# Gates projected beside the attention heads, branch projections after them: one core, one encoder block in float32

## The chip, the cores and the metric

The kernel runs on one core of one Trainium2 chip. The metric is the device time in microseconds; the time of the kernel before is the median of three runs. A profile of one further execution gives the span from the first to the last instruction and, for each engine, what it did when: TensorE (PE, with its weight loads as PEld), VectorE (DVE), ScalarE (ACT), GpSimd (POOL) and SyncE (SP, which here only issues DMAs).

## The reference

One residual layer over 512 tokens of width 1024, with 16 learned meta tokens in front (528 rows, `L`). Cut to what matters here:

```python
xn = rmsnorm(h, norm_mix_g[l])
proj = xn @ w_in[l]                      # stick-breaking q, k, v and differential q, k, v, 8 heads each
...                                      # o_sb: stick-breaking attention; o_df: differential attention, normalised per head
y_sb = o_sb @ w_br_sb[l]                 # "branch projections"
y_df = o_df @ w_br_df[l]
gates = jax.nn.sigmoid(xn @ w_gate[l] + b_gate[l]).reshape(B, L_pad, 2, D)
merged = gates[:, :, 0] * y_sb + gates[:, :, 1] * y_df
h = h + merged @ w_out[l]
hn = rmsnorm(h, norm_ffn_g[l])
h = h + (jax.nn.silu(hn @ w_ffn_gate[l]) * (hn @ w_ffn_up[l])) @ w_ffn_down[l]
```

A gate for output channels f depends on `xn` alone; a branch projection for the same channels needs all eight heads of its branch.

## The kernel before, in words

Activations stand transposed: 128 channels on the partitions, tokens along the free dimension. Every float32 operand of a large product is split in two float32r parts, high (`_h`) and low (`_l`), and `mm3` (lines 284 to 289) computes a product with three matmuls: high x high (L287), high x low (L288), low x high (L289). A weight block of 128x1024 comes from DRAM through SP into one of three staging buffers (`wst`), and is split by ACT (L78, the high part `wh`) and DVE (L79, the low part `wl`) into one of four buffers. `stream` lists all weight blocks in the order of use; `stage` issues loads ahead, `prepare` splits ahead, and `weights(key)` asks for a block, which also drives both. `cols` puts a block of 128 output columns and all 8 input blocks into the stream, `rows` one of 512 output columns and 2 input blocks.

The stages follow each other. First the input is normalised and transposed into `xT_h`, `xT_l`. Then come the 8 stick-breaking heads and the 8 differential heads. While head h runs (its generator yields between its own PE steps), the loop at L1006 interleaves "units": pieces of PE work that prepare head h+1 (q, k, v projections from xT) and more pieces that are independent of the head. `n` in the loop is the number of units between two steps. A full unit for 512 tokens is 12 matmuls of 512 columns. An output larger than a unit is cut in two (`halves`: input blocks 0 to 3, then 4 to 7, into the same PSUM tile).

The further pieces are, before the change:

- at the first two heads, gates 0 of both branches (`gate_out`), kept in DRAM (`g_part`);
- from the third head on, one branch block per head: `y_units(name, i, o)` takes the results of one pair of heads (`o_h`, `o_l`, two heads in one tile), multiplies them with a `rows` block, and gives, for each of four outputs f, a partial sum of six matmuls. ACT copies it from PSUM to `ys`, `gate_tile` or `y_out` (L796), and POOL issues a store to `y_part[name][f]` in DRAM, a plain one for the first pair (L798) and an adding one for the other three (L800);
- at the last head, the gates f = 1 of both branches, and behind it the gates f = 2 and the last two branch blocks.

In the merge (L1111 to L1130) the gates f = 3 to 7 are projected, each branch sum is read back from DRAM by SP (`y_back`, L1067), and gate and branch are multiplied (L1124: POOL for f below 6, DVE otherwise) and added (L1128). `merge_sums` then makes the block sums that the output projection's seven products need, and splits them. The output projection adds into `hres`, which holds x (loaded by L1135); its normalised transposed rows feed the feed-forward part.

The order of instructions on PE, DVE and ACT is written out by hand only at the start. Elsewhere the framework's planner orders the instructions of each engine by the program's order and by its own estimate of when each is ready, gives each tile its memory, and sets the waits. Tiles of one pool and tag share buffers: a new tile of a tag waits until an old one's readers are done. Of these the change touches `xT_h`, `xT_l` and `y_sb` in the pool `xtp` (`tA`, then `y_out`, then `hres` have the tag `y_sb`), the tags `sg0`, `sg1`, `o_h` and `o_l` (two buffers each), and the tags `y_sb` and `y_df` of the merge's pool `mgp`, whose memory is that of the attention's pool `ap_` once this is closed (L1056). PSUM has four tiles (`mm_tile`, `tr_tile`) for all projections and transposes, and two double ones (`z_tile`).

In the differential heads the last step (`norm`, L767 to L776) is put off into the next head (`late`), and for the last head it runs at L1048. During the heads `tick` also issues, on POOL, background DMAs that add up weight blocks in DRAM for later stages.

Of the kernel before, what the change touches and what calls it, by code (L numbers as in the profile page):

```python
# [41 lines left out]
def block_kernel(ctx: ExitStack, tc: tile.TileContext, x, meta, norm_mix_g, w_in, w_gate, b_gate,  # L42
# [45 lines left out]

    for h in range(NH):

        for i in (0, 1, 2) if h < SEVEN else (2, 1, 0):
            cols(("sb", h, i), w_in, i * D + h * P)
        if 0 < h < 3:
            cols(("gate", h - 1, 0), w_gate, (h - 1) * D)
        if h > 2:
            rows(("y_sb", h - 3), w_br_sb, (h + 1) % 2 * 512, (h - 3) // 2 * 2)
    for h in range(NH):
        for i in range(3):
            cols(("df", h, i), w_in, (3 + i) * D + h * P)
        if h < 3:  # L100
            rows(("y_sb", h + 5), w_br_sb, (h + 1) % 2 * 512, (h + 5) // 2 * 2)
        else:
            rows(("y_df", h - 3), w_br_df, (h + 1) % 2 * 512, (h - 3) // 2 * 2)
    rows(("y_df", 5), w_br_df, 512, 4)
    for f in range(1, 3):
        for br in range(2):
            cols(("gate", br, f), w_gate, br * D + f * P)
    for i in range(2):
        rows(("y_df", 6 + i), w_br_df, i * 512, 6)
    for f in range(3, KT):  # L110
        for br in range(2):
            cols(("gate", br, f), w_gate, br * D + f * P)
# [217 lines left out]
    y_count, y_out = [0], []  # L330
# [277 lines left out]
    def sb_head(h, d, o_h, o_l):  # L608
# [48 lines left out]
        nc.vector.tensor_tensor(o_l, ps, o_h.bitcast(F32), op=ALU.subtract)  # L657

# [35 lines left out]
    def df_head(h, d, o_h, o_l):  # L694
# [82 lines left out]

        late.append(norm)


    def y_units(name, i, o):

        def unit(fs):
            wh, wl = weights((name, i))
            for f in fs:
                ps = mm_tile()
                cs = slice(f % 4 * P, (f % 4 + 1) * P)
                mm3(ps, [(wh[:, k, cs], wl[:, k, cs], o[0][:, k], o[1][:, k]) for k in range(2)])
                if y_out:
                    ys = y_out[0][:, y_count[0] % KT]  # L790
                elif y_count[0] % 2:
                    ys = ap_.tile([P, SEQ], F32, tag="ys", bufs=2, name="ys")
                else:
                    ys = gate_tile(0)
                y_count[0] += 1
                nc.scalar.copy(ys, ps)  # L796
                if i < 2:
                    nc.gpsimd.dma_start(y_part[name][f], ys)  # L798
                else:
                    nc.gpsimd.dma_start(y_part[name][f], ys, accum_op=ALU.add)  # L800

        f0 = i % 2 * 4
        return [lambda: unit((f0, f0 + 1)), lambda: unit((f0 + 2, f0 + 3))]
# [7 lines left out]
    g_part = [ydram.tile([P, SEQ], F32, name=f"g_{br}") for br in range(2)]  # L811

    def gate_out(br):
        g = gate_tile(0)
        first, second = gate(br, 0, g, AF.Identity)

        def rest():
            second()
            nc.gpsimd.dma_start(g_part[br], g)

        return [first, rest]
# [183 lines left out]
    todo = []  # L1005
    for br in range(2):  # L1006
        name, head = (("y_sb", sb_head), ("y_df", df_head))[br]
        if br:
            nc.gpsimd.memset(a_s, 0.0)
            y_out.append(xtp.tile([P, KT, SEQ], F32, tag="y_sb", name="y_out"))  # L1010
        for h in range(NH):
# [13 lines left out]
            more = todo.pop(0) if todo else []  # L1025
            if br == 0 and h < 2:
                more = gate_out(h)
# [8 lines left out]
            for n in head(h, d, o[0][:, h % 2], o[1][:, h % 2]):  # L1036
# [6 lines left out]
            if h % 2:  # L1043
                todo += [y_units(name, h - 1 + i, o) for i in range(2)]
    sg1 = [gate_tile(br) for br in range(2)]
    units = gate(0, 2, sg1[0], AF.Identity) + gate(1, 2, sg1[1], AF.Identity)
    units[0]()
    late.pop(0)()  # L1048
    for u in units[1:]:
        u()  # L1050
    for units in todo:
        for u in units:
            u()
    for sg in sg0 + sg1:
        nc.scalar.activation(sg, sg, AF.Sigmoid)
# [7 lines left out]
    def y_back(f):  # L1063
        got = []
        for name in ("y_sb", "y_df"):
            y = mgp.tile([P, SEQ], F32, tag=name, name=name, bufs=2)
            nc.sync.dma_start(y, y_part[name][f])  # L1067
            got.append(y)
        return got
# [41 lines left out]
    merge_order = [1, 2, 0, *range(3, KT)]  # L1111
    ys = [y_back(f) for f in merge_order[:2]]
    for i, f in enumerate(merge_order):
# [418 lines left out]
```

## Time and profile before

| what | value |
|---|---|
| median of three runs | 956.56 us (956.4 to 956.67) |
| profiled execution | 957.57 us |
| its span | 955.8 us |
| mean granted TensorE clock | 0.998 |
| ACT busy, share of the span | 591.7 us (62%) |
| bytes moved by DMA | 158.42 MB, mean 166 GB/s |

How to read it: "busy" is the time in which an engine had at least one instruction running. Matmuls are pipelined, so that the duration of one is longer than the distance of its start from the next one's start; the distance is what a further matmul costs. In the groups of instructions a row gives line, engine, operation, output tile <- inputs, shapes and count, then busy time and the mean ns of one, then the idle time of its engine just before and what ended it. In rows by time the first number is the start in us from the span's start, the second the length in us. The times of a DMA are from issue to landing.

### The profile page before, as it was taken

How to read it: one execution, taken by the hardware profiler on the slowest of the kernel's cores; microseconds unless marked ns; L12 is line 12 of the kernel's file. 1: busy time of each engine (PE TensorE's matmuls, PEld its weight loads, DVE VectorE, ACT ScalarE, POOL GpSimd, SP SyncE). 2: the span in 40 equal slices, each digit the busy share in tenths (PEclk: the TensorE clock that was granted, in tenths of full speed). 3: DMA queues.
4: the chain of work that ended last, by engine and by line, in shares of the span. 5: the costliest groups of instructions: out<-in, count | busy, mean ns of one | idle time of the engine just before them, and what ended most of it. 6: DMA issues, size and time to landing. Idle time of an engine off the chain costs nothing.

```text
span 955.8 us, 16249 instructions
## 1 busy us (share of the span) xinstructions
PE 941.7 (99%) x6105; PEld 851.6 (89%) x6106; DVE 720.4 (75%) x1336; ACT 591.7 (62%) x1137; POOL 190.8 (20%) x212
## 2 busy tenths in 40 slices
PE   8999999999999999999999999999999999999997
PEld 5988989898999899998987888899999999988886
DVE  7978777765677666876662578898888888989875
ACT  6765676666566666666676356765555555666654
POOL 3200121222133343443513530000100000000013
PEclk9999999999999999999999999999999999999999
DMA  8525678778777878799977955517744333276642
GB/s 246 147 66 152 161 178 198 164 166 223 203 180 170 213 170 187 181 198 189 189 197 174 271 190 159 162 42 177 165 118 121 89 113 109 67 244 202 203 154 89
DMA packets 155824, 158.42 MB, mean 166 GB/s; under 512 B 6465, under 2 KB 117218, under 8 KB 155746
## 3 DMA queue, kind: packets, MB, share of 16 engines
q1 hardware_dynamic: 132690, 101.61, 35.3%
q0 software_dynamic: 22896, 55.72, 28.7%
q8 instruction: 48, 0.79, 0.3%
q14 instruction: 30, 0.25, 0.1%
q10 hardware_dynamic: 160, 0.07, 0.0%
HBM read 133.64 MB, written 50.86 MB: 193 GB/s over the span
## 4 chain that ended last, share of the span: by engine, by line
PE 86%; DVE 8%; ACT 2%; DMA 2%; issue 1%; SPq 0%; DVEq 0%; ACTq 0%
PE mm L287 20%; PE mm L288 20%; PE mm L289 20%; PE z L287 6%; PE z L288 6%; PE z L289 6%; DVE wl L79 2%; DMA wsu<-in_w_ffn_up_dram 1%; PE z L705 1%; PE z L704 1%; PE tr L553 1%; PE tr L529 1%; PE z L553 1%; ACT wh L78 1%; DMA slots<-in_w_ffn_down_dram 1%
## 5 line engine op out<-in xcount | busy, mean ns | idle before, releaser
L287 PE MATMUL mm<-xT_h,wh 128*128 128x264 f32 (+2 forms) x656 | 214.6, 327 | 0.5 <-ACT xT_h L909 0.5
L288 PE MATMUL mm<-xT_l,wh 128*128 128x264 f32 (+2 forms) x656 | 213.5, 325 | 0.5
L289 PE MATMUL mm<-xT_h,wl 128*128 128x264 f32 (+2 forms) x656 | 212.6, 324 | 0.0
L79 DVE TENSOR_TENSOR wl<-wst,wh 128x1024 fp32r<-128x1024 f32 (+1 forms) x147 | 164.8, 1125 | 44.7 <-ACT wh L78 44.4
L78 ACT CAST wh<-wst 128x1024 fp32r<-128x1024 f32 (+1 forms) x147 | 141.2, 964 | 83.4 <-PE mm L288 61.9
L288 PEld LDWEIGHTS mm<-xT_l,wh 128*128 128x128 f32 x656 | 123.5, 188 | 10.1 <-DVE xT_l L910 1.3
L287 PEld LDWEIGHTS mm<-xT_h,wh 128*128 128x128 f32 x656 | 123.6, 188 | 10.0 <-ACT xT_h L909 0.9
L289 PEld LDWEIGHTS mm<-xT_h,wl 128*128 128x128 f32 x656 | 123.5, 188 | 10.0
L287 PE MATMUL mm<-hT_h,wh 128*128 128x256 f32 x304 | 86.0, 284 | 0.8 <-ACT qx L1319 0.4
L288 PE MATMUL mm<-hT_l,wh 128*128 128x256 f32 x304 | 86.0, 284 | 0.0
L289 PE MATMUL mm<-hT_h,wl 128*128 128x256 f32 x304 | 85.9, 284 | 0.0
L287 PEld LDWEIGHTS mm<-hT_h,wh 128*128 128x128 f32 x304 | 57.4, 189 | 1.2 <-ACT qx L1319 0.6
L288 PEld LDWEIGHTS mm<-hT_l,wh 128*128 128x128 f32 x304 | 57.6, 190 | 0.0
L289 PEld LDWEIGHTS mm<-hT_h,wl 128*128 128x128 f32 x304 | 57.5, 190 | 0.0
L708 DVE CUSTOM_DVE_ANT_0 pr<-z,bias 128x144 f32<-128x144 f32 (+3 forms) x64 | 30.9, 501 | 35.0 <-PE z L705 34.9
L287 PE MATMUL mm<-o_h,wh 128*128 128x512 f32 x128 | 53.2, 416 | 0.0
L1434 POOL TENSOR_TENSOR outs<-hres,gF 128x512 f32<-128x512 f32 x4 | 6.2, 1551 | 225.5 <-DVE hres L1420 218.0
L288 PE MATMUL z<-wl,da 128*128 128x512 f32 (+1 forms) x132 | 50.4, 382 | 0.5 <-DVE wl L79 0.5
L145 POOL DMA_DIRECT2D ds<-in_w_ffn_down_dram x36 | 30.1, 840 | 102.3 <-ACT wh L78 68.6
L288 PE MATMUL mm<-o_l,wh 128*128 128x512 f32 x128 | 50.2, 392 | 0.3 <-DVE o_l L776 0.3
L287 PE MATMUL z<-wh,da 128*128 128x512 f32 (+1 forms) x132 | 50.3, 381 | 0.0
L289 PE MATMUL z<-wh,da 128*128 128x512 f32 (+1 forms) x132 | 50.2, 380 | 0.0
(375 smaller groups left out, 2557.4 us busy)
## 6 DMA issues: line engine op xcount, KB each, us to landing
wst<-in_w_in_dram SPq DMA_DIRECT2D x40, 512.0 KB, 5.5
ds<-in_w_ffn_down_dram POOLq DMA_DIRECT2D x30, 512.0 KB, 6.1
wst<-in_w_ffn_gate_dram SPq DMA_DIRECT2D x22, 512.0 KB, 3.9
wsu<-in_w_ffn_up_dram SPq DMA_DIRECT2D x20, 512.0 KB, 3.8
wst<-in_w_gate_dram SPq DMA_DIRECT2D x16, 512.0 KB, 6.8
y_df<-y_out POOLq DMA_DIRECT2D x32, 256.0 KB, 7.5
slots<-ds SPq DMA_DIRECT2D x13, 512.0 KB, 3.3
os<-in_w_out_dram POOLq DMA_DIRECT2D x12, 512.0 KB, 5.2
```

Source lines behind the costliest of these rows:

```text
L78: cast["last"] = (hi_copy or nc.scalar.copy)(hi, src)
L79: (lo_eng or nc.vector).tensor_tensor(lo, src, hi.bitcast(F32), op=ALU.subtract)
L145: tc.add_manual_dep(nc.gpsimd.dma_start(dst, src, **kw).ins, cast["last"].ins.name, paced)
L287: nc.tensor.matmul(ps, lhsT=ah, rhs=bh, start=(start and i == 0), stop=False, skip_group_check=skip)
L288: nc.tensor.matmul(ps, lhsT=ah, rhs=bl, start=False, stop=False, skip_group_check=skip)
L289: nc.tensor.matmul(ps, lhsT=al, rhs=bh, start=False, stop=(stop and i == n - 1), skip_group_check=skip)
L529: nc.tensor.transpose(pt[:, j * P:(j + 1) * P], vT[:, j * P:(j + 1) * P], ident)
L553: nc.tensor.transpose(pt[:, (t - j) * P:(t - j + 1) * P], blocks(t, j * P, (j + 1) * P), ident)
L704: nc.tensor.matmul(o, lhsT=q[c][:, qs], rhs=k[c][:, 0, k0:k1], start=True, stop=False)
L705: nc.tensor.matmul(o, lhsT=q[c][:, qs], rhs=k[c][:, 1, k0:k1], start=False, stop=True)
L708: nc.vector.tensor_tensor_reduce(po, zz, bb, scale=1.0, scalar=-3.0e38, op0=ALU.add, op1=ALU.max, accum_out=mx[:, t, c:c + 1])
L1434: nc.gpsimd.tensor_tensor(outs[t][:, D1], hres[:, t, D1], gF[:, D1], op=ALU.mult)
```

## The change

All gates are projected beside the heads, with `gate_out(br, f)`: two units each, evacuated by ACT with the bias added and no sigmoid, and stored to `g_part[br, f]` in DRAM by POOL. One gate stands beside every head except the last differential one; the last stick-breaking head has two. No branch product is made beside the heads. Instead each pair of heads' results is stored to DRAM (`keep`: two stores of 512 KB on POOL) for the stick-breaking pairs and the first two differential pairs; the last two differential pairs stay in SBUF. `back` loads them again with SP: stick-breaking heads 0 to 3 at differential head 4 into the tag `y_sb` of `xtp`, and at the last head stick-breaking heads 4 to 7 into the memory of `xT_h` and differential heads 0 to 3 into that of `xT_l`.

The branch products (`branch`) are now sums over all eight heads for 128 outputs, 24 matmuls into one PSUM tile, in two units. Three of them stand beside the last head and one right behind it; these four are copied to SBUF by ACT. The other twelve stand in the merge, where DVE multiplies them out of PSUM with the gate, which SP has read back (`gate_back`) and ACT has put through the sigmoid. The weight blocks of both branches come as `cols`.

```diff
+    gates = [(br, f) for f in range(KT) for br in range(2)]
...
-        if 0 < h < 3:
-            cols(("gate", h - 1, 0), w_gate, (h - 1) * D)
-        if h > 2:
-            rows(("y_sb", h - 3), w_br_sb, (h + 1) % 2 * 512, (h - 3) // 2 * 2)
+        for _ in range(h > 0):
+            gate_cols()
...
+        for _ in range(1 if h else 2):
+            gate_cols()
...
+    for f in range(6):
+        cols(("y_sb", f), w_br_sb, f * P)
+    for f in range(KT):
+        if f > 5:
+            cols(("y_sb", f), w_br_sb, f * P)
+        cols(("y_df", f), w_br_df, f * P)
...
-    y_part = {n: [ydram.tile([P, SEQ], F32, name=f"{n}_{f}") for f in range(KT)] for n in ("y_sb", "y_df")}
+    g_part = {g: ydram.tile([P, SEQ], F32, name=f"g{g[0]}_{g[1]}") for g in gates}
+    o_part = {(br, p): ydram.tile([P, 2, 2, SEQ], F32, name=f"op{br}_{p}") for br in range(2) for p in range(4 - 2 * br)}
...
     # end of sb_head; in norm() of df_head: if h in (1, 3): keep(1, h // 2, o)
+        if h % 2:
+            keep(0, h // 2, o)
...
-    def y_units(name, i, o):
...
+    def keep(br, p, o):
+        for i in range(2):
+            nc.gpsimd.dma_start(o_part[br, p][:, i], o[i].bitcast(F32))
+
+    def branch(name, f, evac):
+        cell, key = {}, (name, f)
+
+        def part(k0):
+            if k0 == 0:
+                cell["ps"] = mm_tile()
+            wh, wl = weights(key)
+            mm3(cell["ps"], [(wh[:, k], wl[:, k], *head_out[name, k]) for k in range(k0, k0 + 4)], k0 == 0, k0 == 4)
+
+        def second():
+            part(4)
+            with tc.high_priority(offset=EVAC):
+                evac(cell["ps"])
+
+        return [lambda: part(0), second]
...
+    def back(tile, br, p0):
+        for p in range(p0, p0 + 2):
+            for i in range(2):
+                nc.sync.dma_start(tile[:, p - p0, i].bitcast(F32), o_part[br, p][:, i])
...
             if turn is None:
-                sg0 = [gate_tile(br) for br in range(2)]
-                units = more + gate(0, 1, sg0[0], AF.Identity) + gate(1, 1, sg0[1], AF.Identity)
+                back(heads_tile("xT_h"), 0, 2)
+                back(heads_tile("xT_l"), 1, 0)
+                ys = [gate_tile(f % 2) for f in range(4)]
+                u = [branch("y_sb", f, lambda ps, f=f: nc.scalar.copy(ys[f], ps)) for f in range(4)]
+                units = [u[0][0], u[1][0], u[0][1], u[1][1], *u[2]]
             else:
+                more = [u for _ in range(2 if (br, h) == (0, NH - 1) else 1) for u in gate_out(*next(gate_of))]
                 units = units + more[0:1] + [turn] + more[1:]
+            if (br, h) == (1, 4):
+                back(heads_tile("y_sb"), 0, 0)
...
-    sg1 = [gate_tile(br) for br in range(2)]
-    units = gate(0, 2, sg1[0], AF.Identity) + gate(1, 2, sg1[1], AF.Identity)
-    units[0]()
+    u[3][0]()
     late.pop(0)()
-    for u in units[1:]:
-        u()
-    for units in todo:
-        for u in units:
-            u()
-    for sg in sg0 + sg1:
-        nc.scalar.activation(sg, sg, AF.Sigmoid)
+    u[3][1]()
...
+    merge_order = [(0, f) for f in (4, 5, *range(4))]
+    for f in range(KT):
+        merge_order += [(0, f)] * (f > 5) + [(1, f)]
+    gb = [gate_back(*g) for g in merge_order[:2]]
+    firsts = dict(enumerate(ys))
+    for i, (br, f) in enumerate(merge_order):
+        g = gb[i]
+        nc.scalar.activation(g, g, AF.Sigmoid)
+        if i + 2 < len(merge_order):
+            gb.append(gate_back(*merge_order[i + 2]))
+        if br == 0 and f < 4:
+            nc.gpsimd.tensor_tensor(ys[f], g, ys[f], op=ALU.mult)
+            continue
+        for u in branch(("y_sb", "y_df")[br], f, lambda ps: nc.vector.tensor_tensor(g, ps, g, op=ALU.mult)):
+            u()
+        if br == 0:
+            firsts[f] = g
+            continue
...
+        m = mf[:, f] if f < 4 else g
+        nc.vector.tensor_tensor(m, firsts[f], g, op=ALU.add)
         merge_sums(f, m)
```

More of the change, by code (lines that the diff above doesn't have):

```diff
@@ L87, in rows, with gate_cols @@
         stream.append((key, view, c0, 512, k0, k0 + 2))
+    gates = [(br, f) for f in range(KT) for br in range(2)]
+    gate_of = iter(gates)
+    def gate_cols():
+        br, f = next(gate_of)
+        cols(("gate", br, f), w_gate, br * D + f * P)
     for h in range(NH):
@@ L99, in block_kernel @@
             cols(("df", h, i), w_in, (3 + i) * D + h * P)
[L100 to L112, printed above, removed]
+        for _ in range(1 if h else 2):
[6 more added lines that the diff above has]
+        cols(("y_df", f), w_br_df, f * P)
     sums_dram = ctx.enter_context(tc.tile_pool(name="sums_dram", bufs=1, space=bass.MemoryType.DRAM))
@@ L606, in sb_units, with sb_head @@
         return d, q + kv if h < SEVEN else kv[0:3] + q + kv[3:], turn
-    def sb_head(h, d, o_h, o_l):
+    def sb_head(h, d, o_h, o_l, o):
         qh, ql = d["q"]
@@ L692, in block_kernel, with df_head @@
     late = []
-    def df_head(h, d, o_h, o_l):
+    def df_head(h, d, o_h, o_l, o):
         q, k = d["q"], d["k"]
@@ L776, in norm @@
             nc.vector.scalar_tensor_tensor(o_l, of, g_sub, o_h.bitcast(F32), op0=ALU.mult, op1=ALU.subtract)
+            if h in (1, 3):
+                keep(1, h // 2, o)
         late.append(norm)
-    def y_units(name, i, o):
[L783 to L803, printed above, removed]
+    def keep(br, p, o):
+        for i in range(2):
+            nc.gpsimd.dma_start(o_part[br, p][:, i], o[i].bitcast(F32))
+    head_out = {}
+    def branch(name, f, evac):
[10 more added lines that the diff above has]
+        return [lambda: part(0), second]
     def gate(br, f, dst, func):
@@ L809, in gate, with gate_out @@
         return halves(("gate", br, f), xT, QT, evac)
-    g_part = [ydram.tile([P, SEQ], F32, name=f"g_{br}") for br in range(2)]
-    def gate_out(br):
+    def gate_out(br, f):
         g = gate_tile(0)
-        first, second = gate(br, 0, g, AF.Identity)
+        first, second = gate(br, f, g, AF.Identity)
         def rest():
             second()
-            nc.gpsimd.dma_start(g_part[br], g)
+            nc.gpsimd.dma_start(g_part[br, f], g)
         return [first, rest]
@@ L1004, in block_kernel, with heads_tile @@
     turn()
-    todo = []
+    gate_of = iter(gates)
+    def back(tile, br, p0):
+        for p in range(p0, p0 + 2):
+            for i in range(2):
+                nc.sync.dma_start(tile[:, p - p0, i].bitcast(F32), o_part[br, p][:, i])
+            for j in range(2):
+                head_out[("y_sb", "y_df")[br], 2 * p + j] = tile[:, p - p0, 0, j], tile[:, p - p0, 1, j]
+    def heads_tile(tag):
+        return xtp.tile([P, 2, 2, 2, SEQ], F32R, tag=tag, name="ob")
     for br in range(2):
-        name, head = (("y_sb", sb_head), ("y_df", df_head))[br]
+        head = (sb_head, df_head)[br]
         if br:
             nc.gpsimd.memset(a_s, 0.0)
-            y_out.append(xtp.tile([P, KT, SEQ], F32, tag="y_sb", name="y_out"))
         for h in range(NH):
@@ L1035, in block_kernel @@
                     units[i] = lambda a=units[i], b=u: (a(), b())
-            for n in head(h, d, o[0][:, h % 2], o[1][:, h % 2]):
+            for n in head(h, d, o[0][:, h % 2], o[1][:, h % 2], o):
                 for _ in range(min(n, len(units))):
@@ L1042, in block_kernel @@
             d = nd
[L1043 to L1055 removed]
+            if br and h > 3:
+                head_out["y_df", h] = o[0][:, h % 2], o[1][:, h % 2]
+    u[3][0]()
+    late.pop(0)()
+    u[3][1]()
     att.close()
@@ L1061, in block_kernel, with gate_back @@
     mg_l = mgp.tile([P, KT, SEQ], F32R, name="mg_l")
[L1063 to L1069, printed above, removed]
+    def gate_back(br, f):
+        g = mgp.tile([P, SEQ], F32, tag=("y_df", "y_sb")[br == 0 and f > 3], name="gb", bufs=2)
+        nc.sync.dma_start(g, g_part[br, f])
+        return g
     T1, T2 = slice(0, 256), slice(256, 512)
```

20 lines of the change are left out of this document (removed).

## The prediction

> **What bounds the kernel now.** I read the page's busy times first, then busy time by stretch, then what the engines waited for, then the matmuls by shape, and last the order of instructions around head 7. The page and the stretches (stretch: us, then busy us of PE, weight loads, DVE, ACT, POOL, then the granted clock, the DMA share and GB/s):
>
> ```profile
> span 955.8 us, 16249 instructions
> PE 941.7 (99%) x6105; PEld 851.6 (89%) x6106; DVE 720.4 (75%) x1336; ACT 591.7 (62%) x1137; POOL 190.8 (20%) x212
> ...
> 60.00:500.00 440.00, 440.00 (x2844) 397.13 (x2843) 306.77 (x653) 288.84 (x618) 128.90 (x151) 1.00 0.79 183
> 500.00:600.00 100.00, 99.72 (x438) 81.82 (x437) 61.50 (x88) 53.69 (x82) 28.16 (x24) 1.00 0.67 195
> 600.00:660.00 60.00, 57.88 (x431) 54.65 (x430) 51.87 (x93) 38.97 (x76) 2.42 (x3) 1.00 0.46 121
> ```
>
> From 60 to 500 us, where all heads run and where the change removes most, PE is busy 440.00 of 440.00 us at full clock; from 500 to 600 us (rest of the projections, merge, first part of the output projection) it misses 0.28 us. PE is the bound there, and only matmuls saved, or waits of PE removed or added, can move the end. The matmuls of the two projections concerned, by shape:
>
> ```profile
> L287 PE MATMUL mm<-xT_h,wh 128*128 128x512 f32 x248 | 97.6, 394 | 0.0
> L287 PE MATMUL mm<-o_h,wh 128*128 128x512 f32 x128 | 53.2, 416 | 0.0
> ```
>
> The change keeps their number: the branches had 16 weight blocks x 4 outputs x 6 matmuls and have 16 outputs x 24 now, 384 of 512 columns either way, and the gates keep 16 x 24. The 416 ns against 394 ns look like a price of the short sums of six. They are not: what PE waited for in all, and the rows after the last head, say so.
>
> ```profile
> PE mm L288 <- DVE o_l L776: 0.3, 1, 0.3
> ...
> 469.59 0.58 PE L287 MATMUL mm<-o_h,wh 128*128 128x512 f32 x1
> ...
> 496.48 0.59 PE L287 MATMUL mm<-xT_h,wh 128*128 128x512 f32 x1
> ...
> 500.18 0.39 PE L287 MATMUL mm<-xT_h,wh 128*128 128x512 f32 x1
> ...
> 508.14 0.39 PE L289 MATMUL mm<-o_h,wl 128*128 128x512 f32 x1
> 508.41 0.50 PE L287 MATMUL mm<-o_h,wh 128*128 128x512 f32 x1
> 509.20 0.50 PE L288 MATMUL mm<-o_l,wh 128*128 128x512 f32 x1 [0.28 <-DVE o_l L776]
> ...
> 509.77 0.39 PE L287 MATMUL mm<-o_h,wh 128*128 128x512 f32 x1
> ...
> 519.31 0.39 PE L287 MATMUL mm<-xT_h,wh 128*128 128x512 f32 x1
> ...
> 573.71 0.39 PE L287 MATMUL mm<-wh,mg_h 128*128 128x512 f32 x1
> ```
>
> From 519.31 to 573.71, the first matmul of ten gates and the one after their 240th, starts are 54.40 / 240 = 0.227 us apart. Four starts from 508.14 to 509.77 take 1.63 us instead of 0.91: 0.7 us lost once, while PE waits for head 7's result. The other long first matmuls come behind a head's transposes and its last product, where whatever unit stands next pays the same (a branch's at 469.59 has 0.58 us, a gate's at 496.48 has 0.59); the change puts gates in those places and saves nothing.
>
> **The change, part by part.**
>
> *Gates beside the heads, no branch partial sums.* Every head unit of twelve 512-column matmuls gives way to another of twelve. The heads keep their places in time but for two more units at the last stick-breaking head, 24 x 0.227 = 5.4 us, which the part after the heads loses (64 units in both kernels): sum zero. Around it:
>
> ```profile
> L796 ACT COPY y_out<-mm x40: 560/585/590, 284.8 to 520.2; 128x512 f32<-128x512 f32 x40
> L800 POOL DMA_DIRECT2D y_df<-y_out x24: 847/886/1882, 405.9 to 529.2; - x24
> L1120 ACT ACTIVATE sg<-sg 128x512 f32<-128x512 f32 x2 | 1.3, 631 | 2.2 <-DMA sg<-g 2.2
> ```
>
> ACT loses 60 of 64 copies, 60 x 0.585 = 35 us, and gains ten separate sigmoids, 6.3 us. POOL issues 64 accumulating or plain stores of 256 KB less (about 0.9 us each) and 14 gate stores and 12 head stores more. All of it lies beside PE in stretches where PE never waits: 0 us. If that cover were gone, the gate store on POOL would be what the next head's bias and the copies of k wait behind; there is now one a head, and two of heads' results at some, instead of four, so that queue is looser.
>
> *The wait for head 7's result.* Before it, ACT switches tables because early gates are already being turned into sigmoids:
>
> ```profile
> 499.63 1.28 ACT L771 ACT_TABLE_LOAD   x1 [0.80 <-DVE sql L79]
> 503.87 1.28 ACT L772 ACT_TABLE_LOAD   x1
> 505.82 1.28 ACT L1055 ACT_TABLE_LOAD   x1
> 508.39 0.75 DVE L776 SCALAR_TENSOR_TENSOR o_l<-of,g_sub,o_h 128x512 fp32r<-128x512 f32 x1 [1.08 <-ACT o_h L775]
> ```
>
> In the changed kernel no gate can be a sigmoid before the attention's memory is free, which is after this very instruction; the three loads, 3.8 us, leave its path. And head 7's result is first needed at the end of the first y_df sum: after the normalisation's matmuls (500.2, the row at 500.18) come 12 + 24 + 24 + 12 + 9 matmuls, 81 x 0.227 = 18.4 us, so at 518.6 against 509.1. The 0.7 us go: **-0.7 us**. What is late next there is nothing before the loads treated below.
>
> *Heads 4 to 7 of the first branch come back through xT's memory.* This is the added wait. The last reader of xT is now the last gate's second half, which stands where these rows have a branch unit; the unit that first needs heads 4 to 7 stands where they have the first gate of head 7:
>
> ```profile
> 472.31 0.39 PE L289 MATMUL mm<-o_h,wl 128*128 128x512 f32 x1
> ...
> 480.67 0.40 PE L287 MATMUL mm<-xT_h,wh 128*128 128x512 f32 x1
> ...
> 482.06 0.40 PE L287 MATMUL mm<-xT_h,wh 128*128 128x512 f32 x1
> 482.29 0.39 PE L288 MATMUL mm<-xT_l,wh 128*128 128x512 f32 x1
> ```
>
> (All shift by the same 5.4 us.) xT is free at about 472.8. SP then issues four loads of 512 KB for heads 4 to 7 and four more for the second branch. Heads 4 and 5 (two loads) are read from 480.67, heads 6 and 7 (the other two) from 482.06 and 482.29: the fourth must land within 9.5 us. The trace has no such load here; the nearest rows, for time to landing:
>
> ```profile
> slots<-ds SPq DMA_DIRECT2D x13, 512.0 KB, 3.3
> ...
> L1135 POOL DMA_DIRECT2D hres<-in_x_dram x4: 562/580/597, 537.2 to 541.8; - x4
> DMA to landing us min/median/max: 4.1/6.8/8.0
> ...
> DMA packets 5235, 5.53 MB, mean 277 GB/s; under 512 B 210, under 2 KB 4006, under 8 KB 5233
> ```
>
> Good end: one load 3.3 us, three more at the 277 GB/s of 536 to 556 us, 1.9 us each: 9.0 us, landed at 481.8, no wait. Bad end: the four loads of hres, same size, took 541.8 + 8.0 - 537.2 = 12.6 us at most: 485.4, a wait of 3.1 us. I take 10 us, nearer the good end, because the SP queue feeds them back to back and the accumulating stores that shared those microseconds are gone: landed at 482.8, **+0.5 us**. Behind the eight loads on SP (which issues 28 reloads in all instead of 18) stands the weight block of the fifth output: by the good end's rate it lands at 472.8 + 3.3 + 8 x 1.9 = 491.3, and is needed at 500.2 + 12 x 0.227 = 502.9: 0 us.
>
> The Trainium skill (DMA: Bandwidth & Descriptors, "Anatomy of one DMA") gives a transfer as about 2.0 us plus its bytes at 436 GB/s, fitted for DMAs issued from GpSimd. By that, as an estimate from that page, 2 MB would take 6.8 us and the wait would not exist; hres, issued from GpSimd beside other traffic, took up to 12.6 us here, so the trace does not bear it out under load.
>
> *Merge.* What was gate matmuls, two POOL products and an add for each f becomes branch matmuls, a DVE product read from PSUM and the add. Rows of 500 to 620 us:
>
> ```profile
> L79 DVE TENSOR_TENSOR wl<-wst,wh 128x1024 fp32r<-128x1024 f32 x23 | 29.6, 1285 | 13.2 <-ACT wh L78 13.0
> L1209 DVE TENSOR_TENSOR hres<-hres,mm 128x512 f32<-128x512 f32 x10 | 6.8, 682 | 0.0
> ...
> L1128 DVE TENSOR_TENSOR sg<-sg 128x512 f32<-128x512 f32 x4 | 2.8, 692 | 2.4 <-POOL sg L1124 2.4
> L79 DVE TENSOR_TENSOR mg_l<-sg,mg_h 128x512 fp32r<-128x512 f32 x4 | 2.7, 686 | 0.0
> L1096 DVE TENSOR_TENSOR mf<-mf,sg 128x256 f32<-128x256 f32 x4 | 1.7, 424 | 0.1
> L1124 POOL TENSOR_TENSOR sg<-sg,y_df 128x512 f32<-128x512 f32 x6 | 10.5, 1747 | 8.8 <-DMA y_df<-y_df 7.1 <-ACT sg L807 1.7
> y_df<-y_df SPq DMA_DIRECT2D x8, 256.0 KB, 5.1
> ```
>
> POOL drops eight of 12 products, DVE gains eight, 8 x 0.68 = 5.5 us, in a stretch where it is busy 61.5 of 100 us. The tight place is f = 4 and 5, one sum of 24 x 0.227 = 5.4 us of PE each: DVE needs a weight split 1.29, product 0.68, add 0.69, one 512-wide split 0.69 and six 256-wide steps of about 0.42, together 5.9 us. The 1.0 us of both is covered by four PSUM tiles and made up in f = 6, which has 10.9 us of PE: 0 us, 1.0 us if that cover fails. The first product waits for a gate to come back: attention's memory free at 509.1 at the latest, load 5.1, sigmoid 0.63, product 0.68, so 515.5; PE needs that PSUM tile for its fifth sum at 500.2 + 108 x 0.227 = 524.7. Gate loads that wait for a buffer hold back the weight loads behind them on SP, three blocks being staged ahead; 0 us, again.
>
> *The residual's load.* hres now gets its memory when the last y_sb sum's first half is done, 36 matmuls or 8.2 us before the output projection, not at 537. It is wanted 2.7 us into that; by its own rows the last quarter may land 12.6 us after the first issue, 1.7 us late at worst, and then it is DVE that waits, with weight splits prepared three blocks ahead queued behind it. PE reuses that accumulator 8.2 us later: 0 us.
>
> Sum: -0.7 + 0.5 = -0.2 us on the profiled execution of 957.57 us (span 955.8), which is 1.0 us above the median of the runs, 956.56. Carried to the median: **956.4 us**. About 0.2%, 1.9 us, is what a measurement of this kernel can tell from no change, so this is no change.
>
> **The rivals.**
> - *No wait at all.* The loads land within 9.5 us, as the good end says (and the page's formula): -0.7, 955.9 us. Against it: hres's rows.
> - *Slower: the loads for heads 4 to 7 land late.* One place, PE at the third branch unit of head 7. It decides once the fourth load takes over 12.1 us (wait 2.6 less 0.7 is 1.9). At the 12.6 us of hres it gives -0.7 + 3.1, 959.0 us. For it: 4 MB are asked for at once beside POOL's background sums. Against: units that need heads 0 to 3 alone can be put ahead of it.
> - *Slower: DVE in the merge.* The 1.0 of f = 4, 5 and the 1.7 of hres reach PE, with the -0.2: 959.1 us. Against: 38% of DVE is free from 500 to 600.
> - *Faster: looser queues shorten later waits.* PE misses 2.1 us from 600 to 660. Were all of it to go, with the 0.7: 953.8 us. Against: these waits hang on the output projection's residual and the up-projection weights, which the change leaves as they are.
> - *The change moves nothing:* the 0.7 us reappear at another unit: 956.6 us, no change.
>
> **How the numbers follow.** Likeliest case with a short wait, or nothing moved: 0.46. No wait: 0.22. Late loads: 0.16. DVE: 0.06. Faster later: 0.10. Same is 0.46 + 0.22 = 0.68, slower 0.22, faster 0.10. The range runs from 954.9 (between no wait and the faster case) to 959.3 (just past the late loads), leaving out about 0.18; the likeliest case alone spans 955.9 to 957.5.
>
> **What would show it.** Right: the same number of 512-column matmuls, PE busy without a gap from 60 us to head 7, no PE wait on o_l, at most one short wait at the third branch unit of head 7 with a DMA as releaser, no table load between the last head's scores and its o_l. Wrong: a wait of 2.6 us or more on the returned heads, PE waiting for weights or for PSUM in the merge, DVE's hres addition waiting for a DMA with PE idle behind it, or a shorter 600 to 660.

## The result, and the profile after

The changed kernel takes 963.76 us (median of four runs, 962.48 to 964.88) against 956.48 us (955.88 to 956.67) for the kernel before on the same chip: ratio 1.0077, 95% interval 1.0059 to 1.0094. It is slower by 7.3 us, where no change was forecast and a range up to 959.3 us. The profiled execution took 963.38 us, with a span of 961.6 us against 955.8 before.

The page, then busy time by stretch (stretch: us, then busy us of PE, weight loads, DVE, ACT, POOL, the granted clock, the DMA share and GB/s), then what PE waited for (us in all, times, longest):

```profile
span 961.6 us, 16098 instructions
...
PE 944.1 (98%) x6105; PEld 851.6 (89%) x6106; DVE 723.0 (75%) x1344; ACT 565.6 (59%) x1084; POOL 140.1 (15%) x166
```

```profile
60.00:500.00 440.00, 435.75 (x2811) 392.71 (x2810) 302.33 (x645) 263.98 (x564) 99.07 (x121) 1.00 0.72 183
500.00:600.00 100.00, 100.00 (x443) 80.89 (x442) 63.83 (x99) 48.46 (x76) 7.33 (x8) 1.00 0.56 176
600.00:660.00 60.00, 58.70 (x414) 54.55 (x413) 51.50 (x93) 39.74 (x77) 1.49 (x2) 1.00 0.41 112
```

```profile
PE mm L288 <- DMA ob<-op: 2.0, 2, 1.2
...
PE mm L287 <- DMA ob<-op: 1.1, 1, 1.1
PE z L1168 <- DVE hn L1159: 0.8, 1, 0.8
PE z L287 <- DVE a_l L556: 0.8, 1, 0.8
...
PE mm L287 <- ACT qq L443: 0.4, 1, 0.4
```

The number of matmuls is the same, 6105. ACT lost 26 us and POOL 51 us, and PE gained nothing from either. PE was busy in all of the 440 us from 60 to 500 us before; now 4.25 us of them are missing. The wait on `o_l` is no longer among PE's waits. The waits on `ob` (the tiles in which heads' results come back), on `a_l` at L287 and on `qq` are new.

**At head 7.** PE's instructions by time, with the idle time and its releaser in brackets; then the chain that ended last in this stretch, and the line of the reload:

```profile
487.84 0.39 PE L287 MATMUL mm<-ob,wh 128*128 128x512 f32 x1
489.45 0.50 PE L288 MATMUL mm<-ob,wh 128*128 128x512 f32 x1 [1.22 <-DMA ob<-op]
...
490.49 0.39 PE L289 MATMUL mm<-ob,wl 128*128 128x512 f32 x1
491.99 0.49 PE L287 MATMUL mm<-ob,wh 128*128 128x512 f32 x1 [1.12 <-DMA ob<-op]
493.25 0.50 PE L288 MATMUL mm<-ob,wh 128*128 128x512 f32 x1 [0.76 <-DMA ob<-op]
```

```profile
481.38 11.82 DMA ob<-op
493.20 0.04 issue
493.25 0.50 PE mm L288
```

```profile
479.56 4.63 SPq L1011 DMA_DIRECT2D ob<-op  x8
```

The bracket counts idle time only, and a matmul's own length hides a part of a gap. The distance of starts is the price: 1.61, 1.50 and 1.26 us where 0.227 us is usual, so 1.38 + 1.27 + 1.03 = 3.7 us. The last of the four loads landed at 493.2, 13.6 us after the first issue at 479.56. Without the waits PE would have read it at 493.25 - 3.7 = 489.6, 10.0 us after that issue. Of the eight loads in this row the four for the second branch are not needed until 525 us. The chain puts the issue of the last needed load at 481.38, and it is the fifth of the eight: one of the other four stands ahead of it in SP's order.

**The rate on returned heads.** First matmuls of units on returned heads:

```profile
517.04 0.40 PE L287 MATMUL mm<-ob,wh 128*128 128x512 f32 x1
...
525.44 0.40 PE L287 MATMUL mm<-ob,wh 128*128 128x512 f32 x1
```

36 matmuls take 8.40 us, 233.3 ns each, where the gates of the kernel before took 226.7 (54.40 / 240). 288 matmuls read returned heads: 288 x 6.7 ns = 1.9 us.

**The reload of heads 0 to 3.** SP's queue by time, then ACT and PE behind it:

```profile
214.83 1.37 SPq L1011 DMA_DIRECT2D ob<-op  x3
219.52 1.52 SPq L204 DMA_DIRECT2D wst<-in_w_in_dram  x2
221.08 2.73 SPq L1011 DMA_DIRECT2D ob<-op  x1
```

```profile
226.25 1.05 ACT L78 CAST wh<-wst 128x1024 fp32r<-128x1024 f32 x1 [2.31 <-DMA wst<-in_w_in_dram]
```

```profile
228.72 0.39 PE L289 MATMUL mm<-xT_h,wl 128*128 128x512 f32 x1
229.91 0.50 PE L287 MATMUL z<-a_h,vh 128*128 128x512 f32 x1 [0.80 <-DVE a_l L556]
```

The program has this reload at the fifth differential head, some 170 us later. The planner issued it as soon as the memory of `tA` was free (its last reader on PE started at 214.51). The weight block behind it on SP landed late, ACT waited 2.31 us for it, the head's own chain on ACT and DVE ran late, and PE lost 1.19 - 0.23 = 1.0 us.

**One more wait** stands at 155 us. In the chain ahead of it is a load of the attention's constants (`lam`, from 138.78 us on, 7.52 us long). PE's instructions there:

```profile
155.10 0.28 PE L289 MATMUL mm<-xT_h,wl 128*128 128x264 f32 x1
155.74 0.39 PE L287 MATMUL mm<-tA,wh 128*128 128x264 f32 x1 [0.36 <-ACT qq L443]
```

It cost 0.64 - 0.12 = 0.5 us here.

The parts together, in the two profiled executions: -0.7 (`o_l`) + 3.7 + 1.9 + 1.0 + 0.5 - 0.5 = +5.9 us, of 961.6 - 955.8 = 5.8. The last term is from the stretch of 600 to 660 us, where 1.30 us are missing instead of 2.12. Of these 0.8 us only 0.5 are a gain, the wait on `hn` (0.8 us instead of 1.3); the other 0.3 is a wait on `qx` that stands in this stretch before the change and at 663.6 us, behind its end, after it. The medians are 7.3 apart. Of the 1.5 us between the two, 1.1 is the profiled execution of before, which took 957.57 us, that much more than its median; where it spent them is not known. The changed kernel's lies 0.4 under its own. The experiments show what varies between executions.

### The profile page after: what moved, and what is told of

It reads as the page before. It is cut to its first block, busy times and chain, and to the rows that moved or that the text cites. A ratio compares the mean times of both kernels' runs of the same rounds, so it can differ in the third digit from the quotient of the medians.

```text
span 961.6 us, 16098 instructions
## 1 busy us (share of the span) xinstructions
PE 944.1 (98%) x6105; PEld 851.6 (89%) x6106; DVE 723.0 (75%) x1344; ACT 565.6 (59%) x1084; POOL 140.1 (15%) x166
## 4 chain that ended last, share of the span: by engine, by line
PE 83%; DVE 8%; DMA 5%; ACT 3%; issue 1%; SPq 0%; DVEq 0%; ACTq 0%
PE mm L287 19%; PE mm L288 19%; PE mm L289 19%; PE z L287 6%; PE z L288 6%; PE z L289 6%; DVE wl L79 1%; DMA wsu<-in_w_ffn_up_dram 1%; DMA ob<-op 1%; PE z L707 1%; PE z L706 1%; PE tr L553 1%; DMA lam<-in_lam_k_dram 1%; PE tr L529 1%; DMA wst<-in_w_in_dram 1%
## 5 line engine op out<-in xcount | busy, mean ns | idle before, releaser
L287 PE MATMUL mm<-xT_h,wh 128*128 128x264 f32 (+2 forms) x656 | 217.4, 331 | 0.5 <-ACT xT_h L910 0.5
L287 PEld LDWEIGHTS mm<-xT_h,wh 128*128 128x128 f32 x656 | 123.5, 188 | 9.7 <-ACT xT_h L910 0.9
L287 PE MATMUL mm<-hT_h,wh 128*128 128x256 f32 x304 | 85.9, 284 | 0.8 <-ACT hT_h L1173 0.4
L287 PEld LDWEIGHTS mm<-hT_h,wh 128*128 128x128 f32 x304 | 57.3, 189 | 1.2 <-ACT hT_h L1173 0.6
L287 PE MATMUL z<-wh,da 128*128 128x512 f32 (+1 forms) x132 | 50.3, 381 | 0.0
L289 PE MATMUL mm<-t_h,wl 128*128 128x256 f32 x160 | 45.0, 281 | 0.0
L287 PE MATMUL mm<-t_h,wh 128*128 128x256 f32 x160 | 45.0, 281 | 0.0
L288 PE MATMUL mm<-t_l,wh 128*128 128x256 f32 x160 | 44.9, 281 | 0.0
```

The source lines that it names most:

```text
L287: nc.tensor.matmul(ps, lhsT=ah, rhs=bh, start=(start and i == 0), stop=False, skip_group_check=skip)
L288: nc.tensor.matmul(ps, lhsT=ah, rhs=bl, start=False, stop=False, skip_group_check=skip)
L289: nc.tensor.matmul(ps, lhsT=al, rhs=bh, start=False, stop=(stop and i == n - 1), skip_group_check=skip)
```

## The experiments

All of them edit the changed kernel. "Before" is the kernel before, run on the same chip beside each group. Its own median lies between 955.93 and 956.57 us in these groups, and the runs of one kernel up to some 3.5 us apart, so that differences of a microsecond between two medians say little; the traces say more.

| kernel | us | ratio to before | interval |
|---|---|---|---|
| changed | 963.76 | 1.0077 | 1.0059 to 1.0094 |
| e1_offsets | 961.85 | 1.0058 | 1.0040 to 1.0077 |
| e2_no_reload | 958.86 | 1.0024 | 1.0015 to 1.0034 |
| e3_reload_paced | 961.75 | 1.0052 | 1.0035 to 1.0068 |
| e4_lam_on_act | 962.83 | 1.0068 | 1.0051 to 1.0085 |
| e5_ob_aligned | 962.26 | 1.0058 | 1.0042 to 1.0073 |
| e6_no_background | 962.39 | 1.0055 | 1.0040 to 1.0069 |
| e7_second_sum_later | 959.17 | 1.0027 | 1.0018 to 1.0036 |
| e8_all | 955.79 | 0.9993 | 0.9985 to 1.0002 |
| e9_second_four_later | 959.70 | 1.0043 | 1.0030 to 1.0056 |
| e10_contiguous_heads | 960.78 | 1.0045 | 1.0031 to 1.0059 |
| e11_best_order | 956.22 | 0.9998 | 0.9990 to 1.0007 |
| e12_best_contiguous | 955.94 | 0.9992 | 0.9983 to 1.0001 |

### The rate: where the operand begins, or where it came from

The kernel before read most moving operands from `xT`, from its 16th column on (64 bytes into the tile). The tiles `ob` lie in the same memory, and their columns begin at its start. `e1_offsets` gives the three tiles three different starts:

```diff
-        return xtp.tile([P, 2, 2, 2, SEQ], F32R, tag=tag, name="ob")
+        off = {"y_sb": 16, "xT_h": 0, "xT_l": 48}[tag]
+        return xtp.tile([P, off + 8 * SEQ], F32R, tag=tag, name="ob")[:, off:].rearrange("p (a b c t) -> p a b c t", a=2, b=2, c=2)
```

> The tiles that hold the reloaded heads start at other addresses: stick-breaking heads 0 to 3 shifted by 64 bytes (as the projections' operand xT is read, from its 16th column on), heads 4 to 7 not shifted, differential heads 0 to 3 shifted by 192 bytes. In the changed kernel matmuls on all three tiles start 233.3 ns apart (2.80 us for twelve), against 226.7 ns on xT and on heads that never left SBUF. Theory (start address of the moving operand): sums over heads 0 to 3 of the first branch go to 2.72 us for twelve, heads 4 to 7 stay at 2.80, and the third tile, 128 bytes from the good address, tells whether 128 bytes are enough (2.72) or not (2.80). 8 units of twelve at 80 ns less is 0.64 us, 1.3 us with the third tile. Rival (layout with high and low parts in one tile, or that a DMA wrote it, or sums of 24): all three stay at 2.80.

PE by time in `e1_offsets`, in one sum of `y_sb` (twelve matmuls on heads 0 to 3, twelve on 4 to 7):

```profile
555.77 0.39 PE L287 MATMUL mm<-ob,wh 128*128 128x512 f32 x1
...
558.49 0.39 PE L287 MATMUL mm<-ob,wh 128*128 128x512 f32 x1
...
561.29 0.39 PE L287 MATMUL mm<-ob,wh 128*128 128x512 f32 x1
```

Heads 0 to 3, 64 bytes further, take 2.72 us; heads 4 to 7, from the tile's start, 2.80. Heads 0 to 3 of the second branch, 192 bytes further, took 2.79. All three came by the same kind of load, so the place decides. (The whole time fell by 1.9 us where 0.6 was expected; the four runs lie between 960.71 and 963.99.) `e5_ob_aligned` moves all three by 64 bytes and nothing else:

```diff
-        return xtp.tile([P, 2, 2, 2, SEQ], F32R, tag=tag, name="ob")
+        return xtp.tile([P, NM + 8 * SEQ], F32R, tag=tag, name="ob")[:, NM:].rearrange("p (a b c t) -> p a b c t", a=2, b=2, c=2)
```

> All three tiles in which heads' results come back begin 64 bytes further, where the columns of xT begin that the projections read; nothing else moves. Theory (the place at which a moving operand begins sets its rate): all 288 matmuls on returned heads take 2.72 us per twelve instead of 2.80, 288 x 6.7 ns = 1.9 us, so 961.8 us, with the waits at head 7 unchanged. Rival (the rate comes from how the data came there, by a load from DRAM): 2.80 us per twelve stays, 963.8.

First matmuls of the same two units, 288 matmuls apart, in `e5_ob_aligned` and in the changed kernel:

```profile
509.96 0.39 PE L287 MATMUL mm<-ob,wh 128*128 128x512 f32 x1
...
575.24 0.39 PE L287 MATMUL mm<-o_h,wh 128*128 128x512 f32 x1
```

```profile
511.45 0.39 PE L287 MATMUL mm<-ob,wh 128*128 128x512 f32 x1
...
578.21 0.40 PE L287 MATMUL mm<-o_h,wh 128*128 128x512 f32 x1
```

65.28 us instead of 66.76: every matmul at 226.7 ns, and 1.5 us gone in this stretch, where 201 of the matmuls read returned heads (201 x 6.7 ns are 1.3 us); the whole time is 1.5 us shorter. The theory holds.

### The waits at head 7

`e2_no_reload` leaves out the reload of heads 4 to 7: its products read the tile of heads 0 to 3 in their place, so that its result is not the layer's.

```diff
-                back(heads_tile("xT_h"), 0, 2)
+                for k in range(4):
+                    head_out["y_sb", 4 + k] = head_out["y_sb", k]
```

> Heads 4 to 7 of the first branch are not loaded again: their sums read heads 0 to 3 a second time (the output is then not the reference's). Everything else stays. Theory: PE's three waits at the last head, 1.4 + 1.3 + 1.0 = 3.7 us, go with the load, and the time falls from 963.8 to about 960. Rival (PE would wait there for something else, weights or PSUM, or makes the 3.7 us up later): the time stays within 1 us of 963.8.

```profile
60.00:500.00 440.00, 439.93 (x2840) 396.94 (x2839) 305.06 (x648) 266.17 (x568) 99.06 (x121) 1.00 0.72 182
```

No wait on `ob` is left, PE is busy from 60 to 500 us again, and 4.9 us are gone by the medians, more than the 3.7 of the profile (this profiled execution, 956.92 us, is the fastest of its ten and has neither of the waits at 155 and 229 us). What the wait costs in other executions is seen in `e3_reload_paced`, whose own edit concerns the reload of heads 0 to 3:

```diff
-                nc.sync.dma_start(tile[:, p - p0, i].bitcast(F32), o_part[br, p][:, i])
+                load = nc.sync.dma_start(tile[:, p - p0, i].bitcast(F32), o_part[br, p][:, i])
+                if (br, p0) == (0, 0):
+                    paced = mybir.DependencyInfo(mybir.DependencyClass.Sync, mybir.DependencyReason.DATA)
+                    tc.add_manual_dep(load.ins, cast["last"].ins.name, paced)
```

> The four loads of heads 0 to 3 are tied to the weight split of differential head 4, where the program asks for them; in the changed kernel the planner issues them at 215 us, in the last stick-breaking head, as soon as their memory is free, and the weight block behind them on SP lands late. Theory: PE's wait of about 1.0 us for a_l at 229 us goes, and the time falls by about 1 us. Rival (the weight block is late because a gate's block of 512-byte pieces stands before it, not the reload): the wait at 229 us stays.

The wait at 229 us is gone, as expected, and 2.0 us of time (1.0 by the profile); the rival falls, since the gate's block still stands there. But what this wait costs PE changes from execution to execution. In the nine profiled ones with the early reload ACT stands idle for 1.2 to 2.7 us before the split of that weight block, and PE for 0 (`e2_no_reload`, `e5_ob_aligned`) to 1.2 us behind it; in the four with the later reload neither is idle there. At head 7 the loads happened to be later still; stretches and PE by time of `e3_reload_paced`:

```profile
486.00:490.00 4.00, 1.70 (x6) 1.13 (x6) 2.02 (x5) 0.78 (x4) 0.00 (x0) 0.86 1.04 400
490.00:494.00 4.00, 3.19 (x8) 2.20 (x9) 0.00 (x0) 0.55 (x1) 0.00 (x0) 0.50 0.91 315
494.00:498.00 4.00, 4.00 (x17) 3.34 (x16) 1.93 (x4) 2.26 (x5) 0.00 (x0) 0.79 0.13 42
```

```profile
485.05 0.39 PE L287 MATMUL mm<-ob,wh 128*128 128x512 f32 x1
487.21 0.50 PE L288 MATMUL mm<-ob,wh 128*128 128x512 f32 x1 [1.77 <-DMA ob<-op]
...
488.25 0.40 PE L289 MATMUL mm<-ob,wl 128*128 128x512 f32 x1
489.74 0.79 PE L287 MATMUL mm<-ob,wh 128*128 128x512 f32 x1 [1.09 <-DMA ob<-op]
491.33 0.80 PE L288 MATMUL mm<-ob,wh 128*128 128x512 f32 x1 [0.81 <-DMA ob<-op]
...
492.35 0.63 PE L287 MATMUL mm<-ob,wh 128*128 128x512 f32 x1
492.78 0.63 PE L288 MATMUL mm<-ob,wh 128*128 128x512 f32 x1
```

The starts are 1.93, 1.26 and 1.36 us further apart than usual, and the granted clock is 0.50 from 490 to 494. The means beside it say when it fell and rose: 0.86 over 486 to 490 us is 1.1 us of half clock, so it fell at about 488.9, in the second gap, and 0.79 over 494 to 498 us is 1.7 us, so it rose at about 495.7. Between 491.9 and 495.4 starts of 512-column matmuls are 430 ns apart, up to 2 us of loss on top of the waits. `e4_lam_on_act`, which leaves the eight loads as they are, has such a stretch too (0.56 from 492 to 494 us, 0.59 from 494 to 496).

So two things vary between executions. One is the wait itself: in the six profiled executions with the same eight loads in the same order, the changed kernel's among them, the last needed one lands 13.5 to 14.5 us after the first issue, and in the five of these that keep the order of units too, the waits cost 3.7 (changed kernel, `e1_offsets`) to 4.6 us (`e3_reload_paced`). The other is the clock behind it. The changed kernel's profiled execution does not have this stretch; two of its other three runs, of 964.14 and 964.88 us, show a mean clock of 0.994 and 0.996 instead of 0.999, as `e3_reload_paced`'s profiled one does (0.996). The two with 0.999 took 963.38 and 962.48 us. That half clock behind these waits makes the difference is likely from this, not shown. The Trainium skill (TensorE: Matmul & The Clock Gate, "Part 1: The HAM clock gate") gives half speed after an idle window of about 3.4 us; the trace agrees on the half speed, but here the clock fell after a gap of 1.93 us, five matmuls and a part of a second gap, so PE need not stand idle that long without a break. Such gaps don't always do it: in `e5_ob_aligned` three of 1.66, 1.26 and 1.60 us left the clock at 1.00. What decides is open.

What makes the loads late? Four kernels ask one by one. `e7_second_sum_later` moves the reader:

```diff
-                units = [u[0][0], u[1][0], u[0][1], u[1][1], *u[2]]
+                units = [u[0][0], u[1][0], u[2][0], u[0][1], u[1][1], u[2][1]]
```

> Only the order of the units of the last head changes: all three first halves (which need heads 0 to 3 alone) come before any second half, so the returned heads 4 to 7 are first needed 12 matmuls, 2.7 us, later. Theory (late loads of heads 4 to 7 make the wait): PE's wait drops from 3.7 to about 1.0 us, and no stretch of half clock follows, 960.5 to 961 us. Rival (the wait is DMA queueing that moves along with the reader, or the attention's own chain is late next): 3 us or more of wait stay, 963.8.

```profile
492.62 0.40 PE L287 MATMUL mm<-ob,wh 128*128 128x512 f32 x1
493.52 0.50 PE L288 MATMUL mm<-ob,wh 128*128 128x512 f32 x1 [0.51 <-DMA ob<-op]
```

One wait of 0.90 - 0.23 = 0.7 us is left of 3.7, and 4.6 us are gone: the loads don't move along with their reader, and nothing else of the attention was late behind them.

`e6_no_background` takes the background DMAs away from these microseconds:

```diff
-                    tick(*RATE[br])
+                    if br == 0 or h < NH - 2:
+                        tick(*RATE[br])
```

> GpSimd's background sums are not issued during the last two stick-breaking-free (y_df) heads but later, in the FFN; so the four loads of heads 4 to 7 share the DMA engines only with one gate store. Theory (shared bandwidth makes the loads late): the fourth load lands about 10 us after the first issue instead of 13.6, PE's three waits go from 3.7 us to at most 1, 960 us. Rival (the eight queued loads are slow among themselves, 4 MB at once): still 13 us or more, 963.8; the later background work may cost up to 1 us in the FFN.

```profile
491.03 0.50 PE L288 MATMUL mm<-ob,wh 128*128 128x512 f32 x1 [1.68 <-DMA ob<-op]
...
493.44 0.50 PE L288 MATMUL mm<-ob,wh 128*128 128x512 f32 x1 [0.74 <-DMA ob<-op]
```

The fourth needed load landed at 493.4, 12.7 us after the first issue at 480.68: without the background sums it comes 0.9 us sooner than the 13.6, which is no more than these landings differ between executions (13.5 to 14.5). The theory of them as the cause falls. The 1.4 us gained are little more than the spread of the runs.

`e9_second_four_later` makes the other four loads wait for `first_sum[0]`, the copy of the first `y_sb` sum:

```diff
+                if br:
...
+                    tc.add_manual_dep(load.ins, first_sum[0], paced)
...
-                back(heads_tile("xT_l"), 1, 0)
...
+                units = [u[0][0], u[1][0], u[0][1], u[1][1], u[2][0], lambda: (u[2][1](), back(heads_tile("xT_l"), 1, 0))]
```

> The four loads for the second branch (heads 0 to 3 of y_df) are issued only when the first y_sb sum is complete; the four loads that are needed first have the queue to themselves, and the one of the other four that stood ahead of them is gone. GpSimd's background sums stay where they were. Theory (the other four loads make the needed ones late): the fourth needed load lands about 10 us after the first issue instead of 13.6, PE's waits at head 7 go from 3.7 us to at most 1 and the clock stays full behind them, 960 to 961 us. Rival (the loads are slow by themselves, or because of the background sums): waits of 2.5 us or more stay, 963 us or more.

```profile
477.78 1.98 SPq L1011 DMA_DIRECT2D ob<-op  x4
```

```profile
489.16 0.50 PE L288 MATMUL mm<-ob,wh 128*128 128x512 f32 x1 [1.54 <-DMA ob<-op]
```

The last needed load landed 489.1 - 477.8 = 11.3 us after the first issue; of three waits one is left, 1.7 us in distance of starts, where 1 us at most was expected. By the medians 4.1 us are gone, by the ratios to before 3.3; its five runs lie between 959.08 and 962.58, so that the time agrees with the 960 to 961 us expected, and no more can be said.

`e10_contiguous_heads` changes the layout in DRAM, of the stores as of the loads:

```diff
-    o_part = {(br, p): ydram.tile([P, 2, 2, SEQ], F32, ...
+    o_part = {(br, p): ydram.tile([2, P, 2, SEQ], F32, ...
...
-                nc.sync.dma_start(tile[:, p - p0, i].bitcast(F32), o_part[br, p][:, i])
+                nc.sync.dma_start(tile[:, p - p0, i].bitcast(F32), o_part[br, p][i])
```

> The kept heads lie in DRAM so that each 512 KB load reads one contiguous block, instead of 128 pieces of 4 KB at a distance of 8 KB; SBUF side and order stay. Rival theory (the slow first microseconds of the loads, 99 to 260 KB per us, come from the strided source): the loads run at 400 KB per us from the start, the fourth lands after about 9 us, and the wait goes: 960 us. Theory (they come from many loads in flight at once and the other traffic): nothing changes beyond 0.5 us, 963.8 us.

Nothing was expected of it. Stretches from about 1.4 us after the first issue on, in the changed kernel (first issue at 479.56) and in `e10_contiguous_heads` (478.70), GB/s last:

```profile
481.00:483.00 2.00, 2.00 (x10) 1.59 (x9) 2.00 (x9) 1.11 (x5) 1.36 (x2) 1.00 0.80 201
483.00:485.00 2.00, 2.00 (x11) 1.77 (x10) 1.53 (x7) 1.95 (x6) 0.00 (x0) 1.00 0.98 313
```

```profile
480.00:482.00 2.00, 2.00 (x10) 1.62 (x9) 2.00 (x10) 1.25 (x5) 1.44 (x2) 1.00 0.86 322
482.00:484.00 2.00, 2.00 (x11) 1.73 (x10) 1.53 (x9) 1.81 (x6) 0.00 (x0) 1.00 0.97 375
```

```profile
488.82 0.50 PE L287 MATMUL mm<-ob,wh 128*128 128x512 f32 x1 [0.28 <-DMA ob<-op]
490.38 0.50 PE L288 MATMUL mm<-ob,wh 128*128 128x512 f32 x1 [1.06 <-DMA ob<-op]
```

All DMAs of the core together move 322 instead of 201 GB/s at first (166 to 227 over the same two microseconds in the seven other executions with eight strided loads). The last needed load lands 490.4 - 478.7 = 11.7 us after the first issue; by the distance of starts the waits are 0.45 and 1.33 us, 1.8 instead of 3.7, and 3.0 us are gone. So the lateness has two parts of similar size, each found alone: four loads that nobody needs yet (2.3 us of the 13.6) and a source of 4 KB pieces at a distance of 8 KB (1.9 us). The background sums are at most a third, smaller one (0.9 us). Whether the parts add up was not tested, and why a strided source is slow at first the runs don't show. The Trainium skill (DMA: Bandwidth & Descriptors, "Latency and other measured facts") warns of slow copies where the row distance in DRAM is 512 KB and more, and advises a contiguous layout; here the advice helped at a distance of 8 KB.

### The wait at 155 us

`e4_lam_on_act` issues the constants' loads on ACT's queue:

```diff
-            nc.sync.dma_start(lam4[:, i], v.broadcast_to([P, 64]))
+            nc.scalar.dma_start(lam4[:, i], v.broadcast_to([P, 64]))
```

> The four small loads of the lambda vectors are issued from ACT's queue instead of SP's, where in the changed kernel a gate's weight block of 512-byte pieces stands before them (a branch's block of 2 KB pieces in the kernel before) and they land 7.5 us after issue, DVE idle 2.8 us for them. Theory: DVE no longer waits at 144 us, PE's wait of 0.5 us at 155 us goes: 0.5 us less. Rival: they land no sooner, because the DMA engines and not the queue hold them: no change.

The wait is not there, and 0.9 us are gone, within the spread. But it is not there either in `e1_offsets`, `e2_no_reload`, `e3_reload_paced`, `e5_ob_aligned` and `e9_second_four_later`, which leave these loads as they are, while `e6_no_background`, `e7_second_sum_later` and `e10_contiguous_heads` have it. It comes and goes between executions; the experiment settles nothing on its cause.

### All of it undone, and the best version

`e8_all` puts together the edits of `e3_reload_paced`, `e5_ob_aligned`, `e6_no_background` and `e7_second_sum_later`. `e11_best_order` leaves the background sums where they were and has the second branch's loads later instead (`e9_second_four_later`). `e12_best_contiguous` adds the contiguous layout.

> Four edits together: returned heads begin 64 bytes further (-1.9 us), the reload of heads 0 to 3 is issued only in the fifth y_df head (-1.0 us), the third first half comes before the second halves, and no background sums run beside the loads (together -3.7 us, and up to -1 us for the clock that stays full). If these causes are all of the loss: 963.8 - 6.6 to -7.6 = 956.2 to 957.2 us, no measurable difference from the kernel before. If something else costs time as well: 958 us or more.

> Returned heads begin 64 bytes further (-1.5 to -1.9 us), heads 0 to 3 come back only in the fifth y_df head (-1 to -2 us), the third first half comes before the second halves, and the second branch's four loads are issued when the first y_sb sum is complete (no wait at head 7: -3.7 us, and the clock stays full). The background sums stay where they were. If the causes named are all: 955 to 957 us, as the kernel before or up to 0.1% faster (the 0.7 us that the wait on o_l cost). If the later loads make another wait (weights, second branch): 957.5 us or more.

> e11_best_order with the kept heads contiguous in DRAM. If the last waits behind the change are gone already: as e11, 955.5 to 956.5 us, no measurable difference from the kernel before. If faster loads still help a stage behind the heads: up to 1 us faster, 955 us.

Stretch 60 to 500 us in `e11_best_order`:

```profile
60.00:500.00 440.00, 440.00 (x2844) 397.70 (x2843) 305.70 (x649) 266.53 (x571) 98.84 (x121) 1.00 0.72 184
```

All three are back at the time of before (0.9993, 0.9998, 0.9992, each interval holding 1), 7.5 to 8.0 us under the changed kernel, and PE is busy throughout from 60 to 500 us. So the late loads with what follows on them, the place of the operand and the early reload are all of the loss, within about 1 us; the wait at 155 us, which none of these edits touches, is in none of the three profiled executions. How the 7.5 us divide among the causes is known from single executions only. No version beats the kernel before by more than can be measured; the 0.7 us of the `o_l` wait are the only gain that the traces show, and it is too small to be seen in the time.

## Why the prediction was wrong, step by step

- *The wait for heads 4 to 7* is the step that failed first, as a size: the rival "the loads land late" came true, and by more than its worst case (3.1 us). The deadline was right (9.5 us forecast, 10.0 measured from the first issue). The loads were taken to last 10 us, 12.6 at worst; they took 13.6, and the wait was 3.7 us instead of 0.5. The rates came from rows of other loads: SP's loads of 512 KB that land in 3.3 us read a contiguous source, and 277 GB/s was a mean over 20 us, not of the first microseconds behind such a burst, in which all DMAs together ran at 201. The sum counted four loads, though eight were in the same queue, and took for granted that the four came first; SP's order put one of the others ahead. The three tests of this are `e9_second_four_later`, `e10_contiguous_heads` and `e6_no_background`. At its worst this rival gave 959.0 us; the way from there to 963.8 is made of terms that the sum did not have, which follow.
- *"Units that need heads 0 to 3 alone can be put ahead"* stood in the prediction as an argument against this rival. The kernel had only two of its three there, and `e7_second_sum_later` shows what the third was worth: 4.6 us.
- *A wait's price after its end* was not in the sum: `e3_reload_paced` shows half clock for 6.8 us, up to 2 us of loss, from the second of such waits on. It comes in some executions only.
- *"Every head unit of twelve 512-column matmuls gives way to another of twelve ... sum zero"* failed for its rate. The start distance of 0.227 us was carried from `xT` to tiles whose columns begin elsewhere: 0.2333 us, 288 times, 1.9 us (`e5_ob_aligned`).
- *The reload of heads 0 to 3* was not priced, since the program has it in the middle of the second half of the heads. It ran 170 us earlier, ahead of a weight block on SP, for 1.0 us in this execution, 0 to about 1 in others (`e3_reload_paced`). The prediction counted SP's 28 reloads, and looked behind only eight of them.
- *-0.7 us for head 7's result*: right. PE doesn't wait on `o_l`, and no table load stands between the last head's scores and it.
- *ACT and POOL for nothing*: right. 26 us less on ACT and 51 us less on POOL moved nothing.
- *The merge and the residual's load for nothing*: right, PE is busy 100.00 of 100.00 us from 500 to 600.
- *The faster rival* (2.1 us missing from 600 to 660): 0.5 us of it came true in this execution. In `e2_no_reload` and the three last kernels 1.6 to 2.0 us are missing there, near the value of before, so it is not a gain that stays.

## What to carry to other kernels

Where a reload has a deadline, price every load that the queue holds by then, in the queue's real order and with the rate of a load's first microseconds, and first ask whether other work can be put ahead of its reader: that was the largest single gain here, for one line. When an operand moves to another tile, keep the start of its columns as well as its shape. Here a load without a dependency on its place in the program was issued when its memory came free, 170 us early, so tie such a load to the stage that wants it.

## What was not expected of the hardware

- A 512-column matmul whose moving operand begins 64 bytes before, or 128 bytes after, the place from which `xT` is read starts 233 ns after the last one instead of 226.7 (3%); with the same start as `xT` it takes 226.7 ns, whether the data came by DMA or from an engine.
- In one execution a gap of 1.93 us, five matmuls and a part of a second gap were followed by a granted clock of 0.50 for 6.8 us (`e3_reload_paced`); in another, gaps of 1.66, 1.26 and 1.60 us left it at 1.00 (`e5_ob_aligned`).
- With eight loads of 512 KB in one queue, from pieces of 4 KB at a distance of 8 KB, the core's DMAs moved 201 GB/s in the two microseconds from 1.4 us after the first issue on; with the same loads from contiguous blocks 322.
